# A hand-written order of attention on four engines: the turned weights' cast moved ahead of the exponentials, the queries' splits moved into other steps, the bias' scaling moved from VectorE to GpSimd

## The chip, the core and the metric

One core of a Trainium2 chip. The metric is the device time of one execution in microseconds: from the start of the program on the core to its end. Engines are named as the profile names them: PE is TensorE's matrix unit, DVE is VectorE, ACT is ScalarE, POOL is GpSimd, SP is SyncE, which here only issues DMAs.

## What is computed

A two-layer decoder trunk for one sequence of 512 tokens, 1024 features, all in float32. Layer 0 is a gated spatial mixer, a gated feed-forward part with a short convolution, and a gated embedding. Between the layers one K and V (4 heads of 64 features) is made for all later layers. Layer 1 is sliding-window attention over that K and V, then again feed-forward and embedding. The change touches only the attention of layer 1, which in the reference is:

```python
q = (xn @ w_q).reshape(B, nb, BLOCK, N_KV_HEADS, GQA_GROUP, HEAD_DIM)
scores = einsum('bnikgd,bnjkd->bnkgij', q, kblk) * HEAD_DIM ** -0.5
scores = scores - slopes * dist                  # ALiBi, one slope per query head
scores = where(valid, scores, -inf)              # a window of 128 keys
m = maximum(max(scores), sink)                   # sink: one learned logit per head
e = exp(scores - m)
probs = e / (sum(e) + exp(sink - m))
out = einsum('bnkgij,bnjkd->bnikgd', probs, vblk)
return out.reshape(B, S, 1024) @ w_o
```

There are 16 query heads in 4 groups (one per K/V head), and the 512 tokens are 4 blocks of 128. A block's queries see their own block of keys and the block before it; exactly 128 of these 256 keys are in the window.

## The kernel before, in words

**Matrix products in three passes.** [...] A product is three matmuls: high by high (L222), low by high (L223), high by low (L224). The split of a weight costs an ACT cast (`wh`, L187) and a DVE subtraction (`wl`, L196) per unit of 128x1024 numbers. Units come by DMA from SP into raw buffers (`wraw`, L166); during attention only two such buffers are in use. `pump_hi` issues the cast of the next unit, `pump` both halves.

**Attention in 16 steps.** A step i is one head group g and one block n: `steps = [(g, n) ...]`, n fastest, so steps 0, 4, 8 and 12 have n = 0 and no block of keys before them. The stages of a step are spread over three loop bodies, and within a body the order on PE, DVE, ACT and POOL is the written one (`in_order` ties each instruction to the one before it on its engine). In body i, PE does

- the scores of step i (`sc`, 8 matmuls, L741),
- the weights-by-V product of step i-2 (`pv`, 4 matmuls, or 2 where that step has n = 0, L826),
- one unit of "beside" work, then the transposes of the weights of step i-1 (`tr`, 4, L785),
- four more units of beside work.

A unit of beside work is three matmuls of 512 columns: one eighth of a half of the later groups' queries (`project`, 48 units: unit u = 15, 31 or 47 is the last of a group), or a part of the output projection (`merge`). There are 82 of them; body 0 has 7, each later body 5.

DVE does in body i: the choice between the two key blocks (`sc`, L754), scale and bias (`prs`, L755), the extreme over keys (`low`, L760: the logits are kept negated, so the minimum is the maximum of the reference), in some bodies the low half of a weight unit (`wl`), the low half of the turned weights of step i-1 (`pl`, L805), the two sums that make the output of step i-2 (`pb`, L844), which also frees the one PSUM bank that all `pv` share, and the reciprocal of the row sums (L773). ACT does the cast of a weight unit, a copy out of `pv` (L832), the four exponentials (L768), the high half of the turned weights (`ph`, L800), and the casts of the outputs (`oh`, L848). POOL masks the turned weights (L812), multiplies the weights by the reciprocal (L778), and makes the outputs' low halves (L854).

**What else stands in a body.** When a group's half of queries is projected, its split waits in the list `held`; `settle()`, late in the body, issues it: the cast `qh` on ACT (L284), the subtraction `ql` on DVE (L285) and four DMAs on SP that lay the halves out for the scores (L646, L647). Sums of the output projection into the residual (`h`, L876) wait in the same list. After steps 3, 7 and 11 the ALiBi table `alibi` (128x512) is multiplied by a constant for the next group (L915, DVE). The bodies in which a weight unit is split are those in `pumped`.

Of the kernel before, what the change touches and what calls it, by code (L numbers as in the profile page):

```python
# [18 lines left out]
NC = S // P  # L19
# [8 lines left out]
GQ = HEADS // GROUPS  # L28
# [24 lines left out]
def tile_yoco(ctx: ExitStack, tc: tile.TileContext, t, out: bass.AP, out_b: bass.AP):  # L53
    nc = tc.nc
# [98 lines left out]
    state = {"raw": 0, "unit": 0, "next": 0, "tags": list(range(RAWS)), "turn": 0, "cap": held_back}  # L153

    def load(upto, queue=nc.sync):
        while state["raw"] < min(upto, len(units)):
            j = state["raw"]
            a, m, _ = units[j]
            tags = state["tags"]
            r = wp.tile([P, UNIT], F32, tag=f"r{tags[state['turn'] % len(tags)]}", bufs=1, name=f"wraw{j}")  # L160
            state["turn"] += 1
            if len(a.shape) == 4:
                for c in range(2):
                    queue.dma_start(r[:, :m].rearrange("p (k c n) -> p k c n", c=2, n=256)[:, :, c], a[:, :, c])
            else:
                queue.dma_start(r[:, :m], a)  # L166
            raws[j] = r
            state["raw"] += 1
# [3 lines left out]
    def pump_hi(u):  # L172

        _, n, own = units[u]
        load(u + 1)
        if u not in half_done:
            if own:
                pool, *tags = own
                wh, wl = (pool.tile([P, n], F32R, tag=tg, name=f"own{u}_{tg}") for tg in tags)
            else:  # L180
                wh = wp.tile([P, UNIT], F32R, tag="wh", bufs=WBUFS, name=f"wh{u}")
                wl = wp.tile([P, UNIT], F32R, tag="wl", bufs=WBUFS, name=f"wl{u}")
            src = raws.pop(u)[:, :n]
            if u == 0:
                nc.vector.tensor_copy(wh[:, :n], src)
            else:
                nc.scalar.copy(wh[:, :n], src)  # L187
            half_done[u] = wh, wl, n, src
        return True
# [16 lines left out]
    def chunk(cols, kk, ahead=WBUFS):  # L206

        pump(state["next"] + ahead)
        parts = []
        while len(parts) < kk:  # L210
            wh, wl, n = take()
            parts += [(wh, wl, j * cols) for j in range(n // cols)]
        assert len(parts) == kk
        return parts

    def mm3(ps, parts, xs, c0, n=P, first=True, last=True):

        for k, ((wh, wl, off), (xh, xl)) in enumerate(zip(parts, xs)):
            a, b = off + c0, off + c0 + n
            st = first and k == 0  # L220
            en = last and k == len(parts) - 1
            nc.tensor.matmul(ps, wh[:, a:b], xh, start=st, stop=False)  # L222
            nc.tensor.matmul(ps, wh[:, a:b], xl, start=False, stop=False)  # L223
            nc.tensor.matmul(ps, wl[:, a:b], xh, start=False, stop=en)  # L224
# [19 lines left out]
    h = [hp.tile([P, S], F32, tag=f"h{k}", name=f"h{k}") for k in range(KD)]  # L244
# [115 lines left out]
    def slope(hd):  # L360
        return 2.0 ** (-8.0 * (hd + 1) / HEADS)
# [162 lines left out]
    for c in range(NC):  # L524
        vps[1].append(psum(f"v1_{c}"))
        mm3t(vps[1][c], xs, parts, 0, S, c)
        if c == 0:
# [24 lines left out]
                            fill=0.0, base=0, channel_multiplier=-1)  # L552
# [18 lines left out]
    for c in range(4):  # L571
# [4 lines left out]
        for j in range(2):  # L576
            m = 2 * c + j
# [3 lines left out]
            u = tp.tile([P, S], F32, tag="sg", name=f"u{m}")  # L581
# [88 lines left out]
    alibi = at.tile([P, GQ, P], F32, tag="alibi", name="alibi")  # L670
# [25 lines left out]
    box = {}  # L696

    def project(u):

        g, j, k = u // 16 + 1, u // 8 % 2, u % 8  # L700
        if u % 16 == 0:
            box["q"] = chunk(256, KD, ahead=0)
        if k == 0:
            box["qp"] = psum(f"q{g}_{j}", "mm")
        mm3(box["qp"], box["q"][k : k + 1], xq[k : k + 1], j * P, first=k == 0, last=k == KD - 1)
        if k == KD - 1:
            held.append((queries, box["qp"], g, j))

    def merge(m, k0, k1, first, last, ps=None):

        c, half = m // 2, k0 // 4
        if (c, half) not in box:
            box[c, half] = chunk(256, 4, ahead=0)
        if first:
            box[f"o{m}"] = psum(f"o{m}_{half}", "mm") if ps is None else ps
        mm3(box[f"o{m}"], box[c, half][k0 % 4 : (k1 - 1) % 4 + 1], o2[k0:k1], m % 2 * P, first=first, last=last)
        if last:
            if k0 == 3:
                held.append((nc.vector.tensor_add, h[m], h[m], box[f"o{m}"]))
            else:  # L720
                nc.vector.tensor_add(h[m], h[m], box[f"o{m}"])

# [41 lines left out]
    def exps(i, es):  # L764

        pr, low, sm = live[i]
        for e in es:
            nc.scalar.activation(pr[:, e, :], pr[:, e, :], AF.Exp, bias=low[:, e : e + 1], scale=-1.0,  # L768
                                 accum_out=sm[:, e : e + 1])

    def inverse(i):

        nc.vector.reciprocal(live[i][2], live[i][2])  # L773
# [6 lines left out]
    def turn(i):  # L780

        pr = live[i][0]
        tr = psum(f"tr{i}", "tr")
        for e in range(GQ):
            nc.tensor.transpose(tr[:, e * P : (e + 1) * P], pr[:, e, :P], ident)  # L785
        return tr

    def homes(i):

        if i % 2:  # L790
            two = [wp.tile([P, 2, S], F32R, tag=f"r{2 + q}", bufs=1, name=f"p{x}{i}") for q, x in enumerate("pm")]
            return [x[:, a, :] for x in two for a in range(2)]
        one = [ap.tile([P, S], F32R, tag=f"a{x}{SLOTS - 1}", name=f"p{x}{i}") for x in "hl"]
        m5 = mp.tile([P, 2, S], F32R, tag="m5", name=f"pm{i}") if steps[i][1] else one
        return one + ([m5[:, 0], m5[:, 1]] if steps[i][1] else one)

    def turned_hi(i, tr):

        live[i] = homes(i)
        nc.scalar.copy(live[i][0], tr)  # L800
# [53 lines left out]
            eng.tensor_sub(ol, src, oh.bitcast(F32))  # L854

    last = len(steps)
    held = []
    work = [(project, u) for u in range(48)]
    part = lambda m, k: (merge, m, k, k + 1, k == 0, k == 3 and m > 3)
    work += [part(m, k) for m, k in ((4, 0), (4, 1), (5, 0), (5, 1), (6, 0), (6, 1), (4, 2), (4, 3),  # L860
                                             (5, 2), (5, 3), (6, 2), (6, 3))]
    work += [part(m, k) for m in (7, 0, 1, 2, 3) for k in range(4)]
    work += [part(0, 4), part(1, 4)]
    beside = [work[:7]] + [work[5 * i + 2 : 5 * i + 7] for i in range(1, last)]
    assert 5 * last + 2 == len(work)
    pumped = (0, 1, 3, 4, 6, 7, 9, 10, 11, 13, 15)

    def fill(i, a, b):

        for f, *args in beside[i][a:b]:  # L870
            f(*args)

    def settle():

        for f, *args in held:
            f(*args)  # L876
        held.clear()
# [5 lines left out]
    with in_order(*engines):  # L883
        for i in range(last):
            o = scores(i)
            logits(i, o)
            cast = i and i in pumped and pump_hi(state["unit"])
            if i >= 2:
                pv = mix(i - 2)
                low = low_rows(i - 2, pv)  # L890
            if i == 0:
                values(3)
            fill(i, 0, 1)
            if i:
                tr = turn(i - 1)
            if i + 1 < last:
                sinks(i + 1)
            exps(i, (0,))
            if i:
                turned_hi(i - 1, tr)  # L900
            exps(i, (1, 2, 3))
            if cast:
                pump(state["unit"] + 1)
            if i:
                masks(i - 1, (0,))
                turned_lo(i - 1, tr)
                masks(i - 1, (1,))
            if i >= 2:
                pairs = outputs(i - 2, pv, low)
            inverse(i)  # L910
            weights(i)
            if i >= 2:
                output_lows(pairs, nc.gpsimd)
            if i % NC == NC - 1 and i + 1 < last:
                nc.vector.tensor_scalar_mul(alibi, alibi, slope(GQ - 1))  # L915
            fill(i, 1, 4)
            settle()
            if i == 0:
                pump(state["unit"] + 1)
            fill(i, 4, None)  # L920
            load(min(state["unit"] + 2, held_back))
        settle()
        pv = mix(last - 2)
        low = low_rows(last - 2, pv)
        for m in (0, 1):
            merge(m, 5, 6, False, False)
        pairs = outputs(last - 2, pv, low)
        merge(2, 4, 6, False, False)
        tr = turn(last - 1)
        turned_hi(last - 1, tr)  # L930
        masks(last - 1, (0,))
        turned_lo(last - 1, tr)
        masks(last - 1, (1,))
        output_lows(pairs, nc.gpsimd)
# [222 lines left out]
```

## Time and profile before

| | |
|---|---|
| time, median of 3 runs | 1144.59 us (1144.54 to 1144.83) |
| the profiled execution: its own time | 1144.61 us |
| its span, first to last instruction | 1142.9 us |
| mean granted TensorE clock | 0.997 |
| busy: PE, DVE, ACT, POOL | 1124.6, 736.5, 509.7, 136.3 us |
| attention, from the first scores of step 1 to the first `pv` of body 15 | 599.24 to 689.34 us |

The profile is one execution. Its own time is 1.7 us longer than its span, and 0.02 us from the median. A timeline row reads: start, duration, engine, line, operation, output<-inputs, shape, count, and in brackets the idle time before it and what ended that. Ends of matmuls are modelled, so a row of 0.39 us may be followed by the next one 0.23 us later; only starts are used here for PE.

### The profile page before, as it was taken

How to read it: one execution, taken by the hardware profiler on the slowest of the kernel's cores; microseconds unless marked ns; L12 is line 12 of the kernel's file. 1: busy time of each engine (PE TensorE's matmuls, PEld its weight loads, DVE VectorE, ACT ScalarE, POOL GpSimd, SP SyncE). 2: the span in 40 equal slices, each digit the busy share in tenths (PEclk: the TensorE clock that was granted, in tenths of full speed). 3: DMA queues.
4: the chain of work that ended last, by engine and by line, in shares of the span. 5: the costliest groups of instructions: out<-in, count | busy, mean ns of one | idle time of the engine just before them, and what ended most of it. 6: DMA issues, size and time to landing. Idle time of an engine off the chain costs nothing.

```text
span 1142.9 us, 13705 instructions
## 1 busy us (share of the span) xinstructions
PE 1124.6 (98%) x5248; PEld 937.9 (82%) x5248; DVE 736.5 (64%) x983; ACT 509.7 (45%) x808; POOL 136.3 (12%) x169
## 2 busy tenths in 40 slices
PE   9999999999999999999999999999999999999996
PEld 7888888888888888888897788888888888888895
DVE  7356467762677367557857886687735774577656
ACT  6533344441343244445756766554423442344532
POOL 2100210000000000022233453200000000000232
PEclk9999999999999999999999999999999999999998
DMA  9322322322323333332054324432322323332202
GB/s 319 123 82 81 104 88 97 111 92 92 108 71 99 111 110 86 100 111 93 19 147 129 103 65 167 141 107 84 111 92 93 102 73 104 110 97 88 81 13 74
DMA packets 44690, 116.48 MB, mean 102 GB/s; under 512 B 4936, under 2 KB 16848, under 8 KB 44624
## 3 DMA queue, kind: packets, MB, share of 16 engines
q1 hardware_dynamic: 43504, 114.42, 31.6%
q10 hardware_dynamic: 1120, 1.18, 0.3%
q8 instruction: 41, 0.67, 0.2%
q14 instruction: 25, 0.20, 0.1%
HBM read 108.24 MB, written 2.11 MB: 97 GB/s over the span
## 4 chain that ended last, share of the span: by engine, by line
PE 90%; DVE 5%; ACT 2%; issue 1%; POOL 1%; DMA 0%; SPq 0%; POOLq 0%; DVEq 0%; ACTq 0%
PE up L224 14%; PE up L223 14%; PE up L222 14%; PE d L223 8%; PE d L224 8%; PE d L222 8%; PE gate L222 2%; PE gate L224 2%; PE gate L223 2%; PE u L224 1%; PE u L222 1%; PE u L223 1%; PE v L234 1%; PE v L233 1%; PE v L235 1%
## 5 line engine op out<-in xcount | busy, mean ns | idle before, releaser
L196 DVE TENSOR_TENSOR wl<-wraw,wh 128x1024 fp32r<-128x1024 f32 (+2 forms) x197 | 237.5, 1207 | 121.8 <-ACT wh L187 121.2
L187 ACT CAST wh<-wraw 128x1024 fp32r<-128x1024 f32 (+1 forms) x196 | 201.8, 1032 | 235.5 <-PE d L223 135.9
L222 PE MATMUL up<-nf00h,wh 128*128 128x512 f32 x352 | 137.1, 390 | 0.0
L222 PE MATMUL up<-nf10h,wh 128*128 128x512 f32 x352 | 137.0, 389 | 0.0
L224 PE MATMUL up<-nf00h,wl 128*128 128x512 f32 x352 | 137.0, 389 | 0.0
L223 PE MATMUL up<-nf10l,wh 128*128 128x512 f32 x352 | 136.9, 389 | 0.0
L222 PE MATMUL d<-ah,wh 128*128 128x512 f32 x352 | 136.9, 389 | 0.0
L223 PE MATMUL d<-al,wh 128*128 128x512 f32 x352 | 136.9, 389 | 0.0
L224 PE MATMUL d<-ah,wl 128*128 128x512 f32 x352 | 136.9, 389 | 0.0
L223 PE MATMUL up<-nf00l,wh 128*128 128x512 f32 x352 | 136.9, 389 | 0.0
L224 PE MATMUL up<-nf10h,wl 128*128 128x512 f32 x352 | 136.9, 389 | 0.0
L409 ACT ACTIVATE c<-hs,vec 128x512 f32<-128x512 f32 x88 | 71.6, 814 | 88.2 <-DVE hs L405 87.2
L410 DVE SCALAR_TENSOR_TENSOR c<-hs,vec,c 128x511 f32<-128x511 f32 x88 | 65.9, 749 | 37.4 <-ACT c L409 37.2
L383 DVE TENSOR_TENSOR h<-h,d 128x512 f32<-128x512 f32 x56 | 38.5, 687 | 69.0 <-PE d L224 69.0
L284 ACT CAST ah<-a 128x512 fp32r<-128x512 f32 x44 | 27.3, 622 | 113.4 <-DVE a L415 113.4
L222 PEld LDWEIGHTS up<-nf10h,wh 128*128 128x128 f32 x352 | 66.1, 188 | 13.8
L223 PEld LDWEIGHTS up<-nf00l,wh 128*128 128x128 f32 x352 | 66.1, 188 | 13.8
L222 PEld LDWEIGHTS d<-ah,wh 128*128 128x128 f32 x352 | 66.1, 188 | 13.8
L223 PEld LDWEIGHTS d<-al,wh 128*128 128x128 f32 x352 | 66.1, 188 | 13.7
L223 PEld LDWEIGHTS up<-nf10l,wh 128*128 128x128 f32 x352 | 66.1, 188 | 13.7
L224 PEld LDWEIGHTS up<-nf00h,wl 128*128 128x128 f32 x352 | 66.1, 188 | 13.7
L224 PEld LDWEIGHTS d<-ah,wl 128*128 128x128 f32 x352 | 66.1, 188 | 13.7
(316 smaller groups left out, 2027.9 us busy)
## 6 DMA issues: line engine op xcount, KB each, us to landing
wraw<-in_w_up SPq DMA_DIRECT2D x88, 512.0 KB, 3.5
wraw<-in_w_down SPq DMA_DIRECT2D x32, 512.0 KB, 3.6
wraw<-in_w_down SPq DMA_DIRECT2D x16, 384.0 KB, 3.3
wraw<-in_w_u SPq DMA_DIRECT2D x8, 512.0 KB, 6.8
wraw<-in_w_out SPq DMA_DIRECT2D x8, 512.0 KB, 3.7
wraw<-in_w_gate SPq DMA_DIRECT2D x8, 512.0 KB, 4.0
wraw<-in_w_q SPq DMA_DIRECT2D x8, 512.0 KB, 3.5
wraw<-in_w_o SPq DMA_DIRECT2D x8, 512.0 KB, 3.3
```

What stands on the lines that cost most here:

```text
L187: nc.scalar.copy(wh[:, :n], src)
L196: nc.vector.tensor_sub(wl[:, :n], src, wh[:, :n].bitcast(F32))
L222: nc.tensor.matmul(ps, wh[:, a:b], xh, start=st, stop=False)
L223: nc.tensor.matmul(ps, wh[:, a:b], xl, start=False, stop=False)
L224: nc.tensor.matmul(ps, wl[:, a:b], xh, start=False, stop=en)
L233: nc.tensor.matmul(ps, xh[:, s], wh[:, a:b], start=st, stop=False)
L234: nc.tensor.matmul(ps, xl[:, s], wh[:, a:b], start=False, stop=False)
L235: nc.tensor.matmul(ps, xh[:, s], wl[:, a:b], start=False, stop=en)
L284: nc.scalar.copy(hi, src)
L383: nc.vector.tensor_add(h[m], h[m], ps)
L409: nc.scalar.activation(c, hs, AF.Identity, bias=v("conv_b", l * 2 * NJ + col), scale=cw[2])
L410: nc.vector.scalar_tensor_tensor(c[:, 1:], hs[:, : S - 1], cw[1], c[:, 1:], op0=ALU.mult, op1=ALU.add)
```

## The change

In the bodies with a weight split nothing is settled any more. In the others (2, 5, 6, 8, 10, 12) `settle()` comes directly behind `logits`, so behind `low`. The last half of the first projected group (u = 15) is settled where it is projected, in body 2. The high half `ph` of step i-1 is written ahead of all four exponentials of step i, instead of behind the first. The `alibi` multiplication goes to GpSimd, ahead of the sinks and the masks of its body. `pumped` loses the effective entries 6 and 10 and gains 14. The sums into `h` have a list of their own and come one per body at the end. Body 0 has 8 units of beside work and body 15 has 4.

```diff
@@ project
         if k == KD - 1:
             held.append((queries, box["qp"], g, j))
+            if u == 15:
+                settle()
@@ merge
             if k0 == 3:
-                held.append((nc.vector.tensor_add, h[m], h[m], box[f"o{m}"]))
+                sums.append((h[m], h[m], box[f"o{m}"]))
@@
-    beside = [work[:7]] + [work[5 * i + 2 : 5 * i + 7] for i in range(1, last)]
-    assert 5 * last + 2 == len(work)
-    pumped = (0, 1, 3, 4, 6, 7, 9, 10, 11, 13, 15)
+    beside = [work[:8]] + [work[5 * i + 3 : 5 * i + 8] for i in range(1, last)]
+    pumped = (1, 3, 4, 7, 9, 11, 13, 14, 15)
@@ the loop over steps
             logits(i, o)
-            cast = i and i in pumped and pump_hi(state["unit"])
+            if i in pumped:
+                pump_hi(state["unit"])
+            elif i > 1:
+                settle()
...
             if i:
                 tr = turn(i - 1)
+                turned_hi(i - 1, tr)
+            if i % NC == NC - 1 and i + 1 < last:
+                nc.gpsimd.tensor_scalar_mul(alibi, alibi, slope(GQ - 1))
             if i + 1 < last:
                 sinks(i + 1)
-            exps(i, (0,))
-            if i:
-                turned_hi(i - 1, tr)
-            exps(i, (1, 2, 3))
-            if cast:
+            exps(i, range(GQ))
+            if i in pumped:
                 pump(state["unit"] + 1)
...
-            if i % NC == NC - 1 and i + 1 < last:
-                nc.vector.tensor_scalar_mul(alibi, alibi, slope(GQ - 1))
-            fill(i, 1, 4)
-            settle()
+            fill(i, 1, None)
             if i == 0:
                 pump(state["unit"] + 1)
-            fill(i, 4, None)
+            if sums:
+                nc.vector.tensor_add(*sums.pop(0))
             load(min(state["unit"] + 2, held_back))
-        settle()
+        assert not sums and not held
```

**DVE, from the end of body 4 into body 5** (the digits behind a name are the step: `sc5`, `low5`; `ql2_0` is the low half of the first half of group 2's queries). Before:

```order
L773 RECIPROCAL sm4_4907<-sm4_4907 128x4
L285 TENSOR_TENSOR ql2_0_4957<-q2_0_4822,qh2_0_4956 128x512
L754 COPY_PREDICATED sc5_4971<-above_467,sc5_4971 128x4x128
L755 SCALAR_TENSOR_TENSOR prs_4587<-sc5_4971,rq_4382,alibi_4491 128x4x128
L760 TENSOR_REDUCE low5_4982<-prs_4587 128x4
L805 TENSOR_TENSOR pl4_5003<-tr4_4995,ph4_5002 128x512
L844 TENSOR_TENSOR pb3_4990<-pv3_4985,pb3_4990 64x2x128 x2
```

After, at the same place:

```order
L775 RECIPROCAL sm4_4910<-sm4_4910 128x4
L756 COPY_PREDICATED sc5_4964<-above_467,sc5_4964 128x4x128
L757 SCALAR_TENSOR_TENSOR prs_4587<-sc5_4964,rq_4382,alibi_4491 128x4x128
L762 TENSOR_REDUCE low5_4975<-prs_4587 128x4
L285 TENSOR_TENSOR ql2_0_4979<-q2_0_4822,qh2_0_4978 128x512
L807 TENSOR_TENSOR pl4_5004<-tr4_4998,ph4_5003 128x512
L846 TENSOR_TENSOR pb3_4993<-pv3_4988,pb3_4993 64x2x128 x2
```

The queries' low half has moved from ahead of the logits of step 5 to behind its `low`.

**ACT, body 5.** Before:

```order
L284 CAST qh2_0_4956<-q2_0_4822 128x512
L832 COPY pb3_4990<-pv3_4985 64x512
L768 ACTIVATE prs_4587,sm5_4984<-prs_4587,low5_4982 128x129
L800 CAST ph4_5002<-tr4_4995 128x512
L768 ACTIVATE prs_4587,sm5_4984<-prs_4587,low5_4982 128x129 x3
```

After:

```order
L284 CAST qh2_0_4978<-q2_0_4822 128x512
L834 COPY pb3_4993<-pv3_4988 64x512
L802 CAST ph4_5003<-tr4_4998 128x512
L770 ACTIVATE prs_4587,sm5_4977<-prs_4587,low5_4975 128x129 x4
L850 CAST oh0_4794<-pb3_4993 128x128
```

`ph4` now stands ahead of all four exponentials of step 5; it used to stand behind the first, which waits for `low5`.

**ACT, body 15, the last one** (`wh121`, `wh122`: weight units of the output projection). Before:

```order
L187 CAST wh122_5667<-wraw122_5462 128x1024
L832 COPY pb13_5675<-pv13_5670 64x512
L768 ACTIVATE prs_4587,sm15_5666<-prs_4587,low15_5664 128x129
L800 CAST ph14_5686<-tr14_5680 128x512
L768 ACTIVATE prs_4587,sm15_5666<-prs_4587,low15_5664 128x129 x3
```

After:

```order
L187 CAST wh121_5666<-wraw121_5581 128x1024
L834 COPY pb13_5674<-pv13_5669 64x512
L187 CAST wh122_5756<-wraw122_5650 128x1024
L802 CAST ph14_5684<-tr14_5679 128x512
L770 ACTIVATE prs_4587,sm15_5665<-prs_4587,low15_5663 128x129 x4
```

One unit fewer has been split by then, and its cast (issued by the code behind the loop, and placed here by the scheduler) stands ahead of `ph14` and the exponentials of step 15.

More of the change, by code (lines that the diff above doesn't have):

```diff
@@ L856, in tile_yoco @@
     last = len(steps)
-    held = []
+    held, sums = [], []
     work = [(project, u) for u in range(48)]
```

## The prediction, made before the changed kernel ran

> **What bounds the kernel now.** I read the page first, then the chain of waits, then a table of windows over the attention, then the timeline.
>
> ```profile
> PE 1124.6 (98%) x5248; PEld 937.9 (82%) x5248; DVE 736.5 (64%) x983; ACT 509.7 (45%) x808; POOL 136.3 (12%) x169
> ...
> PE 90%; DVE 5%; ACT 2%; issue 1%; POOL 1%; DMA 0%; SPq 0%; POOLq 0%; DVEq 0%; ACTq 0%
> ```
>
> PE bounds nearly everything, and the change takes nothing from it. What can be won lies where the chain leaves PE: 5% of it is on DVE and 2% on ACT, much of that between 600 and 672 us, in the attention. PE's "busy" hides its waits there, since the ends of matmuls are modelled. So I cut the stage at the first scores of bodies 2 to 15; the last window ends at the first `pv` of body 15's tail. Columns: from:to, length, busy time of PE, PEld, DVE, ACT, POOL, clock, DMA.
>
> ```profile
> 604.10:609.46 5.36, 5.36 (x31) 4.45 (x29) 3.21 (x6) 2.85 (x10) 1.18 (x2) 1.00 0.67 196
> 609.46:615.98 6.52, 5.98 (x33) 4.97 (x31) 5.32 (x9) 4.61 (x15) 3.29 (x6) 1.00 0.27 62
> 615.98:622.68 6.70, 6.10 (x33) 5.00 (x31) 6.30 (x12) 5.32 (x19) 4.03 (x8) 1.00 0.31 99
> 622.68:628.45 5.77, 5.77 (x32) 4.91 (x31) 3.50 (x7) 2.92 (x10) 2.56 (x5) 1.00 0.66 183
> 628.45:634.64 6.19, 5.66 (x31) 4.51 (x30) 5.83 (x11) 5.41 (x20) 2.95 (x6) 1.00 0.03 5
> 634.64:640.43 5.79, 5.79 (x32) 4.91 (x31) 4.61 (x8) 3.88 (x11) 2.49 (x6) 1.00 0.60 171
> 640.43:646.74 6.31, 6.10 (x32) 5.00 (x31) 4.57 (x9) 3.42 (x13) 3.16 (x6) 1.00 0.65 175
> 646.74:653.43 6.69, 6.01 (x32) 4.96 (x31) 6.18 (x11) 5.61 (x20) 3.28 (x6) 1.00 0.07 17
> 653.43:658.76 5.33, 5.33 (x31) 4.53 (x30) 4.15 (x8) 3.71 (x9) 2.05 (x5) 1.00 0.63 175
> 658.76:665.20 6.44, 6.03 (x33) 4.97 (x32) 5.83 (x10) 4.75 (x17) 3.75 (x7) 1.00 0.27 84
> 665.20:671.14 5.94, 5.90 (x33) 4.92 (x32) 4.72 (x10) 2.64 (x10) 2.79 (x6) 1.00 0.25 88
> 671.14:677.78 6.64, 6.02 (x33) 4.97 (x32) 6.21 (x11) 5.26 (x19) 3.27 (x6) 1.00 0.00 1
> 677.78:683.08 5.30, 5.30 (x30) 4.45 (x29) 3.55 (x8) 3.13 (x12) 2.61 (x5) 1.00 0.32 99
> 683.08:689.34 6.26, 6.21 (x33) 5.00 (x32) 5.78 (x12) 4.82 (x18) 3.81 (x7) 1.00 0.38 107
> ```
>
> Every body from 2 to 14 gives PE the same work, but for half a `pv` in bodies 2, 6, 10, 14 and narrower scores in 4, 8, 12. Undisturbed, it takes 5.78 us (bodies 5 and 7), or 5.33 with half a `pv` (2, 10, 14). I use 5.78 for 4, 8, 12 too, since none of these is undisturbed. What is above that: 0.74 (body 3), 0.92 (4), 0.86 (6), 0.53 (8), 0.91 (9), 0.66 (11), 0.16 (12), 0.86 (13): **5.64 us of waits**, all that an order can win here. Why they arise is seen at body 5 into 6, in rows of three engines:
>
> ```profile
> 623.37 0.50 ACT L848 CAST oh<-pb 128x128 fp32r<-128x128 f32 x2 [0.40 <-DVE pb L844]
> ...
> 624.38 0.69 DVE L285 TENSOR_TENSOR ql<-q,qh 128x512 fp32r<-128x512 f32 x1 [0.90 <-ACT qh L284]
> ...
> 624.99 0.69 DVE L754 COPY_PREDICATED sc<-above,sc 128x512 f32<-128x512 uint32 x1
> ...
> 627.36 0.41 ACT L768 ACTIVATE prs<-prs,low 128x129 f32<-128x129 f32 x1 [2.03 <-DVE low L760]
> ...
> 627.88 0.59 ACT L800 CAST ph<-tr 128x512 fp32r<-128x512 f32 x1
> ...
> 628.50 0.69 DVE L805 TENSOR_TENSOR pl<-tr,ph 128x512 fp32r<-128x512 f32 x1 [1.17 <-ACT ph L800]
> ...
> 629.11 0.84 DVE L844 TENSOR_TENSOR pb<-pv,pb 64x256 f32<-64x256 f32 x2
> ...
> 630.09 0.47 PE L826 MATMUL pv<-ph,vt 128*128 128x512 f32 x1 [0.53 <-DVE pb L844]
> ```
>
> DVE loses time twice. It waits 0.90 us for `qh` ahead of the next logits, and 1.17 us for `ph`, which stands behind an exponential that needs `low`. `pb` therefore ends at 629.95, and PE's next `pv`, which needs the bank that `pb` frees, starts 0.14 later, at 630.09.
>
> **The change, part by part.** Whether the waits go is a race of DVE against PE. DVE in body 6, with a weight split and no queries' split ahead of it, and two rows on PE's pace:
>
> ```profile
> 630.07 0.67 DVE L754 COPY_PREDICATED sc<-above,sc 128x512 f32<-128x512 uint32 x1
> ...
> 632.31 1.22 DVE L196 TENSOR_TENSOR wl<-wraw,wh 128x1024 fp32r<-128x1024 f32 x1
> 633.57 0.69 DVE L805 TENSOR_TENSOR pp<-tr,pp 128x512 fp32r<-128x512 f32 x1
> 634.18 0.83 DVE L844 TENSOR_TENSOR pb<-pv,pb 64x256 f32<-64x256 f32 x2
> ...
> 678.92 0.70 DVE L754 COPY_PREDICATED sc<-above,sc 128x512 f32<-128x512 uint32 x1 [0.33 <-PE sc L741]
> ...
> 684.03 0.47 PE L826 MATMUL pv<-pp,vt 128*128 128x512 f32 x1
> ```
>
> From a body's first scores, T, the logits can start at T+1.14 (677.78 to 678.92) and `pb` is done 4.94 later (630.07 to 635.01); with 0.14 for the signal the next `pv` is free at T+6.22. PE asks for it 0.95 behind the next first scores (683.08 to 684.03): at T+6.73, or T+6.28 after half a `pv`. So **with a weight split DVE is 0.51 us early, or 0.06 in body 14**. With a queries' split in its place (0.69 for 1.22) it is 1.04 early, 0.59 in bodies 6 and 10.
>
> *Queries' splits behind `low`* (bodies 2, 5, 6, 8, 10): the 0.90 wait for `qh` and the 0.69 ahead of the logits go; `ql` fills time in which DVE had nothing to do.
>
> *`ph` ahead of the exponentials*: the 1.17 goes, since the transposes end before `low` does. What is late next is `ql` or `wl`, already in the sum. The four exponentials then wait for `ph`, 0.59 long; only the reciprocal and POOL's product wait for them (third rival).
>
> *u = 15 in body 2*: that body has two queries' splits, and the second still stands ahead of body 3's logits. `pb` ends at T+5.55, and from there to the logits it takes 1.71, as above from 623.28 to 624.99 (`oh` starts 0.09 behind `pb`). So the logits come at T+7.26 instead of T+6.50 (5.36+1.14): 0.76 late, 0.51 of it covered. **0.25 us stays in body 4.** Their DMAs:
>
> ```profile
> L647 SPq DMA_DIRECT2D q<-ql x16: 461/587/1300, 583.3 to 656.4; - x16
> ...
> DMA to landing us min/median/max: 2.2/2.3/3.0
> ```
>
> Behind `ql`, SP issues three more at 0.59 (1.30 at worst), and the last lands 2.3 later: T+10.7 to 11.5. Its scores are due at T+11.7 (5.36+5.78+0.6): no wait, by little. Other queries' DMAs are due a body or more later.
>
> *`alibi` on POOL*, in bodies 3, 7 and 11. DVE loses 0.40 each, which the sum above does not contain. POOL has no such row:
>
> ```profile
> L915 DVE TENSOR_SCALAR alibi<-alibi 128x512 f32<-128x512 f32 x3 | 1.2, 397 | 0.0
> ...
> L729 POOL TENSOR_SCALAR alibi<-dist x4: 636/1034/1165, 21.2 to 24.1; 128x128 f32<-128x128 f32 x4
> ...
> 598.22 1.04 POOL L778 TENSOR_TENSOR prs<-prs,sm 128x512 f32<-128x512 f32 x1 [1.96 <-DVE sm L773]
> ...
> 598.90 1.44 DVE L196 TENSOR_TENSOR wl<-wraw,wh 128x1024 fp32r<-128x1024 f32 x1 [0.76 <-ACT wh L187]
> ...
> L812 POOL TENSOR_SCALAR_AFFINE_SELECT pm<-pp 128x512 fp32r<-128x512 f32 x16 | 10.2, 635 | 20.4 <-ACT pp L800 19.7
> ```
>
> Bounds: 0.64 us (L812, the same size) to 4.1 (four times L729's quarter). I take 1.04, L778's, the nearest in size. It starts at T+2.7, when the biased logits are done, and ends at T+3.75; behind it stand the sinks, the masks and the product, none due before T+6. At 1.04 POOL costs nothing by itself. But it meets `wl`, due at T+3.38 (632.31 less 630.07, plus 1.14). A `wl` beside L778 took 1.44 instead of 1.22. I add 0.25 to each of the three; 0.51 covers it in bodies 7 and 11, nothing does in body 3: **0.25 us more in body 4.**
>
> [...]
>
> *Sums into `h`*: the same four, one a body:
>
> ```profile
> L876 DVE TENSOR_TENSOR h<-h,o 128x512 f32<-128x512 f32 x4 | 2.6, 670 | 0.0
> ```
>
> In bodies 11 and 13 they follow `wl`: 4.94+0.20+0.67 = 5.81 against 5.78. Nothing. The units of beside work number 82 as before: PE's sum is unchanged. In body 15 the cast of a late unit stands ahead of `ph`; its DMA may hold ACT. I count nothing, and up to 0.8 in the range. The loads of the next stage wait one split longer, behind PE work of several us: nothing.
>
> **Sum**: 5.64 less 0.50 is 5.1 us. From the profiled execution's 1144.61 (span 1142.9 and 1.7 around it), which is the median of the runs within 0.02: **1139.5 us**.
>
> **The rivals.** (1) *POOL is slow*: at 4.1 us `alibi` ends at T+6.8, the sinks (0.2) and two masks at T+8.27. The last row of `pv` needs them at T+7.43: 0.84 us in three bodies, 2.5 in all: 1142.0. For it: L729. Against it: L729's rows ran while DVE worked too, and the other 128x512 rows take 0.64 and 1.04.
>
> (2) *The bank stays last*: `wl` and `ql` stand ahead of `pl` and `pb`, so if each DVE body grows by 1.0 us (three rows blocked for 0.33) beside a POOL that works at other moments than before, the six bodies with a weight split whose margin is 0.51 cost 0.49 each and body 14 costs 0.94: 3.9 in all, 1143.4. For it: the margins are small. Against it: in body 14 of before, with nothing ahead of its logits, DVE waits for PE (678.92, 0.33).
>
> (3) *The exponentials wait for PE*, and it gets slower: they now follow `ph`, which follows the transposes, which follow the product of the step before on POOL, which follows its exponentials: a loop. Transposes 0.4, `ph` 0.6, exponentials 1.8, reciprocal 0.4, product 1.2: 4.4 us against 5.33 to 5.78. It decides from 0.9 us more; at 6.4 us each of 14 bodies gains 0.6 over PE's pace: 1144.6-5.6+8.4 = 1147.4. For it: ACT runs in order. Against it: the sum.
>
> The change doing something other than it says isn't one: the order of the instructions was read above.
>
> **How the numbers follow.** Forecast 0.80, (1) 0.08, (2) 0.08, (3) 0.04. Low end: all 5.64, 0.2 for the narrow scores and 0.2 in body 15: 1138.6. High end: POOL's upper bound, 1142.0. A measurement tells 0.2% (2.3 us) from no change; (2) lies within it, and half of (1) may: faster 0.84, same 0.12, slower 0.04.
>
> **What would show it.** Right: bodies near 5.78 and 5.33 but for body 4 (some 6.2); `pl` no longer waits for `ph`; PE's wait for `pb` all but gone; the stage ends 5 us earlier and everything behind keeps its length. Wrong: POOL's `alibi` rows over 2 us, exponentials ended by `ph`, bodies still at 6.2 and more, or a wait of PE behind the attention that wasn't there.

## The result and the profile after

The changed kernel takes **1139.31 us** (median of 5, 1138.97 to 1139.68) against 1144.59 (median of 5, 1144.54 to 1145.04) of the kernel before: a ratio of 0.9953, 95% interval 0.9938 to 0.9967. That is 5.28 us less; 1139.5 was forecast, inside 1138.6 to 1142.0. Its profiled execution has a span of 1137.5 us and a granted clock of 0.997, as before.

First the page: the busy times, and the shares of the chain by engine.

```profile
PE 1122.8 (99%) x5248; PEld 938.6 (83%) x5248; DVE 733.6 (64%) x980; ACT 509.2 (45%) x808; POOL 145.1 (13%) x172
...
PE 95%; DVE 1%; issue 1%; POOL 1%; ACT 1%; DMA 1%; SPq 0%; POOLq 0%; ACTq 0%; DVEq 0%
```

PE's work is the same, DVE's 5% of the chain has become 1%. Then the windows from first scores to first scores, bodies 2 to 15 (from:to, length, busy time of PE, PEld, DVE, ACT, POOL, clock, DMA).

```profile
604.88:610.21 5.33, 5.33 (x31) 4.53 (x29) 4.43 (x9) 3.55 (x13) 2.38 (x4) 1.00 0.51 151
610.21:615.98 5.77, 5.77 (x33) 4.91 (x32) 4.63 (x8) 4.68 (x14) 4.27 (x7) 1.00 0.59 136
615.98:621.92 5.94, 5.92 (x33) 4.93 (x32) 5.72 (x11) 4.26 (x14) 4.53 (x8) 1.00 0.26 99
621.92:627.68 5.76, 5.76 (x32) 4.91 (x31) 4.49 (x10) 3.94 (x15) 2.01 (x5) 1.00 0.52 148
627.68:633.01 5.33, 5.33 (x30) 4.54 (x29) 3.96 (x7) 3.58 (x13) 3.21 (x6) 1.00 0.34 80
633.01:638.78 5.77, 5.77 (x33) 4.91 (x32) 4.70 (x9) 4.18 (x13) 4.90 (x8) 1.00 0.23 54
638.78:644.49 5.71, 5.71 (x33) 4.86 (x31) 4.76 (x10) 3.88 (x14) 3.44 (x7) 1.00 0.49 146
644.49:650.26 5.77, 5.77 (x33) 4.91 (x32) 4.07 (x6) 4.11 (x13) 2.02 (x4) 1.00 0.12 30
650.26:655.55 5.29, 5.29 (x31) 4.49 (x29) 4.65 (x10) 3.81 (x13) 3.18 (x6) 1.00 0.51 151
655.55:661.34 5.79, 5.79 (x33) 4.91 (x32) 5.32 (x10) 4.17 (x13) 4.94 (x8) 1.00 0.23 56
661.34:667.05 5.71, 5.71 (x32) 4.85 (x31) 5.03 (x11) 3.63 (x15) 3.49 (x8) 1.00 0.21 82
667.05:672.82 5.77, 5.77 (x33) 4.91 (x32) 4.76 (x8) 3.76 (x12) 1.94 (x4) 1.00 0.03 6
672.82:678.14 5.32, 5.32 (x30) 4.53 (x29) 4.93 (x9) 4.29 (x13) 3.76 (x6) 1.00 0.25 94
678.14:684.27 6.13, 6.13 (x34) 4.94 (x32) 5.55 (x12) 5.18 (x15) 3.80 (x6) 1.00 0.54 192
```

All bodies now have PE's own length, 5.77 or 5.33, and 5.71 with narrow scores (8, 12); only body 4 is longer, by 0.23. What became of the place that the prediction took apart, body 5 into 6, is seen in the timeline:

```profile
625.92 0.68 DVE L807 TENSOR_TENSOR pl<-tr,ph 128x512 fp32r<-128x512 f32 x1
626.52 0.84 DVE L846 TENSOR_TENSOR pb<-pv,pb 64x256 f32<-64x256 f32 x2
...
628.63 0.40 PE L828 MATMUL pv<-ph,vt 128*128 128x512 f32 x1
628.83 0.70 DVE L756 COPY_PREDICATED sc<-above,sc 128x512 f32<-128x512 uint32 x1 [1.26 <-PE sc L743]
```

`pl` waits for nothing, `pb` ends at 627.36, 1.27 ahead of the `pv` that needs its bank, and DVE then waits 1.26 for PE's scores. Before, PE waited for DVE here.

### The profile page after: what moved, and what is told of

It reads as the page before. It is cut to its first block, busy times and chain, and to the rows that moved or that the text cites. A ratio compares the mean times of both kernels' runs of the same rounds, so it can differ in the third digit from the quotient of the medians.

```text
span 1137.5 us, 13704 instructions
## 1 busy us (share of the span) xinstructions
PE 1122.8 (99%) x5248; PEld 938.6 (83%) x5248; DVE 733.6 (64%) x980; ACT 509.2 (45%) x808; POOL 145.1 (13%) x172
## 4 chain that ended last, share of the span: by engine, by line
PE 95%; DVE 1%; issue 1%; POOL 1%; ACT 1%; DMA 1%; SPq 0%; POOLq 0%; ACTq 0%; DVEq 0%
PE up L222 14%; PE up L224 14%; PE up L223 14%; PE d L224 8%; PE d L222 8%; PE d L223 8%; PE gate L222 2%; PE gate L223 2%; PE gate L224 2%; PE q L222 1%; PE q L224 1%; PE sc L743 1%; PE q L223 1%; PE u L222 1%; PE u L224 1%; PE u L223 1%
## 5 line engine op out<-in xcount | busy, mean ns | idle before, releaser
L224 PEld LDWEIGHTS up<-nf10h,wl 128*128 128x128 f32 x352 | 66.1, 188 | 13.7
```

## The experiments

None of the twelve kernels leaves out a part of the reference. "Alone" kernels start from the kernel before, "undone" ones from the kernel after. Before, run beside them on the same chips, took 1144.68 to 1144.76 us. The lengths of bodies below are read from the timelines, first scores to first scores; bold is 0.2 or more above PE's own length.

| kernel | time, us | 3 | 4 | 6 | 7 | 8 | 9 | 10 | 11 | 12 | 13 |
|---|---|---|---|---|---|---|---|---|---|---|---|
| before | 1144.59 | **6.52** | **6.70** | **6.19** | 5.79 | **6.31** | **6.69** | 5.33 | **6.44** | **5.94** | **6.64** |
| e1 ph alone | 1140.97 | 5.77 | **6.22** | 5.31 | 5.76 | **6.48** | 5.79 | 5.32 | **6.45** | 5.72 | 5.76 |
| e2 queries alone | 1141.96 | 5.84 | **6.69** | 5.33 | **6.30** | 5.70 | 5.77 | 5.32 | **6.31** | **5.98** | **6.60** |
| e11 both, old schedule | 1140.00 | 5.76 | **6.24** | 5.33 | **6.29** | 5.72 | 5.76 | 5.33 | **6.33** | 5.71 | 5.77 |
| e3 schedule alone | 1144.88 | **6.54** | **6.68** | **6.19** | **6.99** | 5.72 | **6.09** | 5.32 | **6.76** | 5.72 | **6.00** |
| e4 ph undone | 1140.46 | 5.83 | **6.67** | 5.32 | 5.82 | 5.71 | 5.75 | 5.43 | 5.76 | 5.72 | 5.76 |
| e5 queries undone | 1139.10 | 5.77 | 5.76 | 5.32 | 5.77 | 5.71 | 5.77 | 5.29 | 5.78 | 5.79 | 5.77 |
| after | 1139.31 | 5.77 | **5.94** | 5.33 | 5.77 | 5.71 | 5.77 | 5.29 | 5.79 | 5.71 | 5.77 |

**e1: ph alone.** In the kernel before:

```diff
-            exps(i, (0,))
             if i:
                 turned_hi(i - 1, tr)
-            exps(i, (1, 2, 3))
+            exps(i, range(GQ))
```

> The kernel before with one edit: the high half of the turned weights is written ahead of all four exponentials. Theory (DVE against PE, a margin per body): in a body with a weight split the 1.22 us of wl cover the 1.17 us that pl waits for ph, so the edit wins nothing there (bodies 3, 7, 10, 11: the waits in the bodies behind them, 0.92, 0.53, 0.66 and 0.16, stay). In the bodies without one (2, 5, 8, 12) it wins the 1.17, and the waits of bodies 3, 6, 9 and 13 (0.74, 0.86, 0.91, 0.86: 3.4 together) go. So 1141.2 us, 1140.6 to 1142.0. Rival 1 (the gain comes from where the weight splits stand): within 0.5 of 1144.6. Rival 2 (this move is the whole gain): 1139.3.

1140.97 us (ratio 0.9966, 0.9954 to 0.9979), inside the range. The waits of bodies 3, 6, 9 and 13 are gone and 11's is there, as the theory has it; 12's 0.16 went too. Bodies 4 and 8 still wait, but not for the theory's reason alone. Body 4 has 0.51 over 5.71 (0.99 before), and `wl` of the weight split ahead of it takes 1.66 instead of 1.22, beside a mask on POOL that started 0.05 ahead:

```profile
613.71 0.63 POOL L812 TENSOR_SCALAR_AFFINE_SELECT pm<-ph 128x512 fp32r<-128x512 f32 x1 [1.34 <-ACT ph L800]
613.76 1.66 DVE L196 TENSOR_TENSOR wl<-wraw,wh 128x1024 fp32r<-128x1024 f32 x1
```

In body 8 (0.77 over 5.71, 0.60 before) PE stands 0.39 in the scores for the DMA that lays out `ql`, until 639.85; `pb` comes last all the same, at 640.12. One moved cast is worth 3.7 of the 5.3 us, and what it wins lies behind the bodies without a weight split.

**e2: the queries' splits alone.** In the kernel before:

```diff
             logits(i, o)
+            if i > 1:
+                settle()
...
-            settle()
+            for s in sums:
+                nc.vector.tensor_add(*s)
+            sums.clear()
```

> The kernel before with one part of the change: the queries' splits go directly behind low (u = 15 stays in body 2), the sums into h keep their place in a list of their own, all else is as before. Theory: DVE is no longer late for the logits; ql fills 0.69 of the 1.17 wait for ph where no weight is split. In bodies 3, 6, 7 and 10 ql and wl then stand in one body, and DVE ends 0.69 later than with wl alone: against margins of 0.51 (0.06 behind the short bodies 6 and 10) that is 0.2 in 4 and 8 (0.25 more in 4 for u = 15) and 0.6 in 7 and 11, some 1.9 us in all of the 5.64. So 1140.9 us, 1140.3 to 1141.7. Rival 1 (the gain comes from where the weight splits stand): within 0.5 of 1144.6. Rival 2 (the move of ph is the whole gain): 1144 and more.

1141.96 us (0.9977, 0.9968 to 0.9986), 0.3 above the range. 7 and 11 wait about as worked out (0.5 each, against 0.6), and the 0.2 of body 8 did not come. Body 4 waits 0.98 against 0.45: `pp` of body 2 still waits 0.64 for its high half, as in e4 below, and that moves the logits of body 3. 12 waits 0.27 and 13 still 0.83, which the estimate had left out: body 12 has neither a weight split nor queries' splits, so nothing fills the wait of `pl` for `ph`, and two sums into `h` and the bias stand at the end of body 11.

**e3: the schedule alone.** The kernel after with the three moves undone; the places of units, weight splits and sums remain.

```diff
-            elif i > 1:
-                settle()
...
-                turned_hi(i - 1, tr)
-            if i % NC == NC - 1 and i + 1 < last:
-                nc.gpsimd.tensor_scalar_mul(alibi, alibi, slope(GQ - 1))
...
-            exps(i, range(GQ))
+            exps(i, (0,))
+            if i:
+                turned_hi(i - 1, tr)
+            exps(i, (1, 2, 3))
...
+                nc.vector.tensor_scalar_mul(alibi, alibi, slope(GQ - 1))
-            fill(i, 1, None)
+            fill(i, 1, 4)
+            settle()
+            fill(i, 4, None)
```

> The kernel after with three parts undone: ph behind the first exponential, the queries' splits at the end of the body, the bias' multiplication on DVE. What is left of the change is where units of beside work and weight splits stand and the sums into h one by one. Theory: logits late by 0.6 to 0.9 and pl by 1.17 in bodies 2, 5, 6, 8 and 10, together about 1.8 to 2.1 against a margin of 1.73 without a weight split (1.28 behind short bodies 2, 6, 10): 0.3 to 0.8 in each of the bodies 3, 6, 7, 9, 11 and 0.3 in body 4. So 1142.3 us, 1141.3 to 1143.5. Rival (the gain comes from this schedule): 1139.3 to 1139.7.

1144.88 us (1.0002, 0.9992 to 1.0011): no gain at all. The rival falls; the theory's figure was 2.6 too low. The kernel of before shows why: its logits of body 5 stand at T+2.31 (624.99 less 622.68), 1.17 late, not the 0.6 to 0.9 that I had used, and 1.17 for `ph` comes on top.

**e4: ph undone** (the exponentials' lines as in e3, nothing else).

> The kernel after with one part undone: ph behind the first exponential again. Theory: with the queries' splits behind low, pl is late by 1.17 less 0.69 in the bodies with ql (0.48 against 1.04, 0.59 behind the short ones), not at all behind wl, and by 1.17 in body 12 (against 1.73). No margin is used up: 1139.3 us, 1139.0 to 1139.7, all bodies at the lengths of the kernel after. Rival 2 (the move of ph is the gain, or half of it): 1142 to 1144.6, with waits of 0.5 to 0.9 in most bodies.

1140.46 us (0.9963, 0.995 to 0.9976): 0.8 above the range, and nearly all of it in one body. DVE in bodies 2 and 3 of e4, then of the kernel after (the timeline):

```profile
609.63 0.69 DVE L807 TENSOR_TENSOR pp<-tr,pp 128x512 fp32r<-128x512 f32 x1 [0.64 <-ACT pp L802]
...
612.18 0.69 DVE L285 TENSOR_TENSOR ql<-q,qh 128x512 fp32r<-128x512 f32 x1 [0.90 <-ACT qh L284]
612.79 0.69 DVE L756 COPY_PREDICATED sc<-above,sc 128x512 f32<-128x512 uint32 x1
```

```profile
611.43 0.69 DVE L285 TENSOR_TENSOR ql<-q,qh 128x512 fp32r<-128x512 f32 x1 [0.90 <-ACT qh L284]
612.04 0.69 DVE L756 COPY_PREDICATED sc<-above,sc 128x512 f32<-128x512 uint32 x1
```

The 0.64 that `pp` waits in body 2 moves the second queries' split and the logits of body 3 from 612.04 to 612.79, and body 4 grows by 0.73. Elsewhere the margins hold, as expected; I had forgotten that body 3 has none left.

**e5: the queries' splits undone** (as the `settle` lines of e3, and no `settle` in `project`).

> The kernel after with one part undone: the queries' splits at the end of a body again, ahead of the next logits (ends of bodies 1, 2, 4, 5, 7, 9). Theory: with ph ahead of the exponentials, logits that come 0.8 to 1.2 late are covered where no weight is split (margin 1.73, 1.28 behind a short body), and the only weight split behind a late one is that of body 3. The kernel with ph alone has the same three splits around body 3 and waits 0.51 in body 4, against 0.23 in the kernel after. So 0.3 more: 1139.6 us, 1139.2 to 1140.0. Rival (the queries' move has a gain of its own, in each of six bodies): 1141 and more, waits in bodies 6, 9 and 11.

1139.10 us (0.9949, 0.9933 to 0.9965): 0.1 below the range, and no slower than the kernel after; the 0.3 more that was worked out from e1 did not come (e10 shows why). With `ph` moved and the weight splits placed as they are, the queries' move wins nothing; body 4 is even 0.18 shorter, since `u = 7` no longer stands in the middle of body 2.

**e6: the bias on DVE.**

```diff
-            if i % NC == NC - 1 and i + 1 < last:
-                nc.gpsimd.tensor_scalar_mul(alibi, alibi, slope(GQ - 1))
...
+            if i % NC == NC - 1 and i + 1 < last:
+                nc.vector.tensor_scalar_mul(alibi, alibi, slope(GQ - 1))
```

> The kernel after with one part undone: the bias' multiplication on DVE, behind the reciprocal of bodies 3, 7 and 11. Theory: 0.40 at the end of DVE's body makes the logits of bodies 4, 8 and 12 that much later at most, against margins of 0.44 (weight split and narrow scores), 0.97 and 1.66: 1139.3 us, 1139.0 to 1139.6, bodies 5, 9 and 13 at 5.76 to 5.86. Rival (DVE's time is what is short, so the 1.2 us count): 1140.5.

1139.83 us (0.9955, 0.9941 to 0.997), 0.2 above the range; bodies 5, 9 and 13 at 5.76 to 5.77, as the theory has it, but body 4 at 6.23, which neither theory has. The timeline of body 3, POOL and DVE:

```profile
613.57 0.63 POOL L814 TENSOR_SCALAR_AFFINE_SELECT pm<-ph 128x512 fp32r<-128x512 f32 x1 [1.38 <-ACT ph L802]
613.78 1.50 DVE L196 TENSOR_TENSOR wl<-wraw,wh 128x1024 fp32r<-128x1024 f32 x1
```

The mask starts 0.21 ahead of `wl`, and `wl` takes 1.50 instead of 1.22. In the kernel after, POOL is busy with the bias then, and the mask comes later. e10 tests that.

**e10: bias on DVE, and a multiplication by 1.0 on POOL at the old place** (one line more than e6).

```diff
+                nc.gpsimd.tensor_scalar_mul(alibi, alibi, 1.0)
```

> The kernel with the bias' multiplication on DVE, and at the place where POOL had it a multiplication by 1.0 on POOL. In the kernel with the multiplication on DVE, body 4 waited 0.52 instead of 0.23, and wl in body 3 took 1.50 instead of 1.22 beside POOL's mask that had started 0.2 ahead of it. Theory (the multiplication on POOL is worth something because it holds that mask back until wl is done): wl in body 3 takes 1.22 again and body 4 5.94 to 6.0. Rival (what counts is DVE's 0.40): body 4 stays at 6.23.

1139.15 us (0.9954, 0.994 to 0.9967), body 4 at 5.95. The same place:

```profile
613.23 1.49 POOL L902 TENSOR_SCALAR alibi<-alibi 128x512 f32<-128x512 f32 x1 [1.10 <-DVE prs L757]
613.85 1.22 DVE L196 TENSOR_TENSOR wl<-wraw,wh 128x1024 fp32r<-128x1024 f32 x1
...
615.07 0.63 POOL L814 TENSOR_SCALAR_AFFINE_SELECT pm<-ph 128x512 fp32r<-128x512 f32 x1
```

`wl` is back at 1.22 and body 4 at its length, though DVE does the 0.40 in three bodies. So DVE's 1.2 us cost nothing; POOL's multiplication was worth 0.29 us in body 4 because it keeps the mask off `wl`. The mask became able to meet `wl` when `ph` moved ahead: 0.44 of the 0.51 that body 4 waits in e1 is this stretch of `wl`. In e5 POOL has the bias and `wl` takes 1.22, so e1's 0.51 was the wrong thing to reckon e5 from.

**e7: a dose for the margins.** `pl` is subtracted twice:

```diff
         nc.vector.tensor_sub(pl, tr, ph.bitcast(F32))
+        nc.vector.tensor_sub(pl, tr, ph.bitcast(F32))
```

> The kernel after with the subtraction pl done twice in every body (same data, 0.62 us more of DVE each): a dose for the margins. Theory (margins 0.44 to 0.51 with a weight split, 0.06 behind body 14, 1.0 with a queries' split and 0.59 behind short ones, none in body 3): waits of 1.4 in body 4 (now 0.23; bodies 2 and 3 add up), 0.1 to 0.2 each in 5, 8, 10, 12 and 14, 0.6 in the tail of 15, next to nothing in 6, 7, 9, 11. Some 2.7 us: 1142.0, 1141.2 to 1142.9. Rival 1 (DVE is as full as PE: each body pays in full): 8 us, 1147.4. Rival 2 (margins over 0.62 everywhere): 1139.3.

1145.40 us (1.0008, 0.9999 to 1.0017), 2.5 above the range. The dose was larger than meant: in body 7 the two rows start at 639.11 and 639.82, 0.71 apart. Against the kernel after, the first `pv` of bodies 8, 10, 12 and 14, each behind a weight split, starts 0.23, 0.12, 0.33 and 0.12 later in its body: 0.38 to 0.59 of the dose was covered. The bodies themselves grow by 0.27, 0.32, 0.34 and 0.29; what they have beyond the wait comes behind the `pv`. Bodies 5, 6, 9, 11 and 13 grow by nothing or 0.02 at most, body 7 by 0.11, body 2 by 0.19, body 4 by 1.28, and in body 15 the first `pv` comes 1.1 later (there `wl` of body 14 took 1.60, beside a mask). So neither rival: there are margins, and they are small. Some 2 us more arise behind the loop, which no theory had. There the last transposes (693.68) are followed directly by the `pv` that needs their weights (694.96), where eight other matmuls stand between the two in the kernel after (688.40 to 690.31). Why the order differs is open; the whole time of e7 is therefore no measure of the margins.

**e9: the bias three times on POOL.**

```diff
                 nc.gpsimd.tensor_scalar_mul(alibi, alibi, slope(GQ - 1))
+                nc.gpsimd.tensor_scalar_mul(alibi, alibi, 1.0)
+                nc.gpsimd.tensor_scalar_mul(alibi, alibi, 1.0)
```

> The kernel after with the bias' multiplication on POOL followed by two more by 1.0: POOL's price three times, at the same place. Theory A (1.49 us is the operation's own price on POOL): 4.47 us; in body 3 it ends at T+7.9, the masks at T+8.8 and T+9.4, so body 4 grows to 7.9; in bodies 7 and 11 the masks end at T+8.05 and T+8.7 against a need at T+6.97 and T+7.43, so bodies 8 and 12 grow to 7.0. Together 4.6 us: 1143.9, 1143.0 to 1144.8. Theory B (its own price is near 0.64 and DVE beside it stretches it): the two more take 0.64 each, all three 2.8: bodies 4, 8 and 12 grow by 0.2 at most, 1139.6.

1145.54 us (1.0009, 1.0 to 1.0018; its executions scatter from 1144.48 to 1146.88), 0.7 above the range. The rows of the tile `alibi` (ns, minimum, median and maximum of three):

```profile
L902 POOL TENSOR_SCALAR alibi<-alibi x3: 1489/1492/1493, 614.1 to 664.0; 128x512 f32<-128x512 f32 x3
L903 POOL TENSOR_SCALAR alibi<-alibi x3: 1611/1613/1614, 615.6 to 665.6; 128x512 f32<-128x512 f32 x3
L904 POOL TENSOR_SCALAR alibi<-alibi x3: 1488/1488/1489, 617.3 to 667.3; 128x512 f32<-128x512 f32 x3
```

Theory A: the third runs while DVE waits for it, and takes 1.49 all the same, so that is its own price. In the profiled execution bodies 4, 8 and 12 grow to 9.51, 7.39 and 7.41, where 7.9, 7.0 and 7.0 were expected; what body 4 has beyond that is told in the last section.

**e11: both moves, old schedule** (e1's and e2's edits together).

> The kernel before with ph ahead of the exponentials and the queries' splits behind low, while the weight splits, the sums into h and the units of beside work stay where they were. Theory (where wl and ql stand in one body DVE is too long by 0.2 to 0.6, whatever the order inside): of the waits with the queries' move alone (0.98 in body 4, 0.53 in 7, 0.53 in 11, 0.27 in 12, 0.83 in 13) that of 13 goes and that of 4 falls by 0.5, the others stay: 1140.6 us, 1140.2 to 1141.2. Rival (the two moves add up, the schedule is worth nothing): 1139.3.

1140.00 us (0.996, 0.9945 to 0.9976): 12 and 13 are mended, 4 in part, and 7 and 11 wait 0.5 as with e2. There `ql` and `wl` stand in one body (6 and 10), and neither move mends that. So the total is 0.2 below the range. The rest of the change wins 0.7 us on this kernel: 1.06 in bodies 7 and 11 by the schedule, 0.30 in body 4, less 0.59 that is lost behind the loop (told at e8). The 0.30 is the place of the bias: as in e6, `wl` of body 3 takes 1.50 here beside the mask. Alone the schedule won nothing.

**e8 and e12: the leftovers mended.** In both a weight split in body 12 as well; in e8 `settle` also in body 1, in e12 the queries' splits as in e5.

```diff
-    pumped = (1, 3, 4, 7, 9, 11, 13, 14, 15)
+    pumped = (1, 3, 4, 7, 9, 11, 12, 13, 14, 15)
...
-            elif i > 1:
+            if i == 1 or i not in pumped:
                 settle()
```

> The kernel after with its two leftovers mended: settle also in body 1 (the split of u = 7 leaves body 2), and a weight split in body 12 as well (the unit that was split behind the loop is then split in body 15, and the embedding's units are loaded and cast earlier). Theory: body 4 at 5.71 instead of 5.94; the wait of 0.47 at the embedding's first matmuls, whose low halves DVE ended late, goes; the split in body 12 uses up to 0.2 in the tail of 15. So 1138.75 us, 1138.4 to 1139.1. Rival (the split in body 12 with the sum into h behind it is one too many: DVE 5.81 against 5.71 in 12, and so on to 14): waits of 0.3 or more in 13 to 15, 1139.3 and more.

> The kernel after with the queries' splits at the end of their bodies again and a weight split in body 12 as well. Theory: body 4 at 5.76 as with the queries' splits undone, no wait of 0.47 at the embedding's first matmuls: 1138.6 us, 1138.2 to 1139.1, as fast as with both leftovers mended. Rival (the queries' move is worth something once all else is mended): 1139.1 and more.

e8 takes 1138.59 us (0.9948, 0.9934 to 0.9962), e12 1138.43 (0.9947, 0.9934 to 0.9959): both 0.7 to 0.9 below the kernel after, and as fast as each other within their scatter (1138.20 to 1139.36, 1138.24 to 1138.61). Body 4 is 5.73 and 5.76; in e8 body 2 is 0.07 longer instead. The second leftover lies behind the loop, at the embedding's first matmuls. First of the kernel before, where nothing waits, then after, then e8 (timeline):

```profile
698.38 0.28 PE L222 MATMUL o<-own_m,wh 128*128 128x256 f32 x1
...
701.18 0.28 PE L222 MATMUL pin<-own_m,wh 128*128 128x256 f32 x1
```

```profile
690.12 1.05 ACT L187 CAST wh<-wraw 128x1024 fp32r<-128x1024 f32 x1
...
691.69 1.48 DVE L196 TENSOR_TENSOR wl<-wraw,wh 128x1024 fp32r<-128x1024 f32 x1
...
692.63 0.28 PE L222 MATMUL o<-own_m,wh 128*128 128x256 f32 x1
692.74 0.28 PE L223 MATMUL o<-own_m,wh 128*128 128x256 f32 x1
693.22 0.39 PE L224 MATMUL o<-own_m,wl 128*128 128x256 f32 x1 [0.20 <-DVE wl L196]
...
696.02 0.28 PE L222 MATMUL pin<-own_m,wh 128*128 128x256 f32 x1
```

```profile
685.90 1.05 ACT L187 CAST wh<-wraw 128x1024 fp32r<-128x1024 f32 x1
...
692.40 0.28 PE L222 MATMUL o<-own_m,wh 128*128 128x256 f32 x1
...
695.20 0.28 PE L222 MATMUL pin<-own_m,wh 128*128 128x256 f32 x1
```

From `o` to `pin` it is 2.80 us before, 3.39 after, 2.80 in e8. With one split more inside the loop the embedding's unit is cast at 685.90 instead of 690.12, its low half is there in time, and 0.59 us come back.

## Why the prediction was right, point by point

**The waits.** 5.64 us of waits in bodies 3 to 13, made by DVE and mended by the order: right, in size and in place. The undisturbed lengths were 5.77 and 5.33. For bodies 4, 8 and 12 they are 5.71, so 0.07 each was won beyond what was counted. One thing was overlooked, in body 4 of the kernel before (timeline):

```profile
617.27 0.30 PE L741 MATMUL sc<-kh,q 128*128 128x128 f32 x1 [0.51 <-DMA q<-ql]
...
617.77 0.47 PE L826 MATMUL pv<-ph,vt 128*128 128x512 f32 x1
```

The scores themselves waited, for the DMA of a queries' half that was split late: they went on 0.68 later than in the kernel after. `pb` ended at 617.62 and still came last, so the account of 5.64 holds, but a second wait lay hidden behind it. In e1 it shows in body 8; in the kernel after, e2, e3, e5 and e11 no scores wait 0.1 or more for this DMA.

**Two causes.** Both delays were real, but they are not two gains. e1 and e2 win 3.7 and 2.7 by themselves, e11 4.7; in the final schedule the queries' move is worth nothing (e5) and that of `ph` 1.15 (e4). A body without a weight split has room for one delay, not for two; a body with one hides the wait for `ph` behind `wl`. The prediction gave the sum rightly and did not see that either cause could be left in nearly everywhere.

**The margin of 0.51 with a weight split.** About right. In the kernel after, `pb` ends, with the 0.14 for the signal, 0.49, 0.51 and 0.59 us ahead of the first `pv` of bodies 8, 12 and 14; e7 gives 0.38 to 0.59. In body 10 it is only 0.25, since DVE stands idle for 0.46 ahead of `low` of step 9, for a reason that the profile doesn't show. In body 15 it is 0.15 where 0.06 was worked out.

**u = 15 in body 2: 0.25 us in body 4.** 0.23 was measured, with some luck. `ql` waits 0.90 for `qh` at 611.43 and the logits of body 3 start at 612.04, T+7.16 against T+7.26 worked out: 0.69 late instead of 0.76. With the 0.49 of body 8 as the room, 0.20 is left; `pv` comes 0.18 later than in body 8. e5 and e8 show the better wording: two queries' splits in body 2 are one too many; with one, body 4 has 0.02 to 0.05.

**The bias on POOL: 1.04 us and 0.25 for a collision.** This step failed in both numbers. The operation takes 1.49, and the collision did not come (the timeline of the kernel after, body 3):

```profile
613.66 1.49 POOL L902 TENSOR_SCALAR alibi<-alibi 128x512 f32<-128x512 f32 x1 [1.10 <-DVE prs L757]
614.29 1.22 DVE L196 TENSOR_TENSOR wl<-wraw,wh 128x1024 fp32r<-128x1024 f32 x1
615.12 0.43 POOL L748 COPY prs<-nsink 128x4 f32<-128x4 f32 x1
```

`wl` ran 0.86 us beside the multiplication, which ended at 615.15, and took its usual 1.22. What was late is POOL's own next row, the sinks: 0.43 instead of 0.19, ended at 615.55, 0.04 behind `wl`. In e6 it was `wl` that took 0.28 longer, behind a mask that had 0.42 left. The 0.25 was taken from the product L778: beside it, lead and stretch of `wl` together are 0.90 (598.22, 598.90 and 0.22 longer). Beside the multiplication they are only 0.47 (last section), and here it started 0.63 ahead. POOL needs 1.49 for what DVE did in 0.40. POOL had the time, so the price was without effect; the place on POOL helped by chance (e6, e10).

**Sums into h, body 15: nothing.** Right: bodies 12 and 14, behind those with a sum and a split, are 5.71 and 5.32, and PE's gap at the last `pv` of body 15 is 0.14 (0.21 before).

**The loads of the next stage: nothing, behind PE work of several us.** This step failed: 0.59 us. I looked at how long PE had work, and not at what stands ahead of the late unit's cast on ACT and of its subtraction on DVE: `pp`, the other unit, and then 1.48 us of `wl`.

**The sum.** From the first scores of body 0 to the embedding's `o` it is 107.69 us before (590.69 to 698.38) and 101.84 after (590.79 to 692.63): 5.85 less. 5.64, 0.21 for the narrow scores and less 0.23 make 5.62 of it; the rest is in gaps of under 0.1. Then 0.59 goes back: 5.26, and 5.28 was measured. That the forecast of 5.1 was so near is in part luck: one loss too many (0.25) and gains not counted (0.2) stood against a loss that was overlooked (0.59).

**The rivals.** POOL at 4.1 us or more does cost what was said and more (e9: with 4.6 us the bodies 4, 8 and 12 grow by 1.7 to 3.6, since the logits of the next body wait for the bias too). The bank comes last again from some 0.4 to 0.6 us more of DVE (e7); the second rival's 1.0 us a body, three rows blocked for 0.33, was my assumption and no run shows it: beside a mask or the multiplication `wl` was stretched by at most 0.44 (e1). The third rival's wait did appear, in the kernel after too (body 5):

```profile
624.72 0.69 DVE L762 TENSOR_REDUCE low<-prs 128x4 f32<-128x516 f32 x1
625.12 0.59 ACT L802 CAST ph<-tr 128x512 fp32r<-128x512 f32 x1 [0.55 <-PE tr L787]
625.60 0.41 ACT L770 ACTIVATE prs<-prs,low 128x129 f32<-128x129 f32 x1
```

`ph` waits 0.55 for PE's transposes, and the exponentials follow it, 0.19 behind the end of `low`; in bodies 4, 7, 8, 11, 12 and 13 it is 0.12 to 0.34. It cost nothing: these bodies keep PE's length, but for what body 4 has from elsewhere. So of the signs of being wrong two came up, exponentials released by `ph` and a new wait of PE behind the attention, and only the second cost time.

## What to carry to other kernels

Lay out the race that sets a stage per step: when the fast engine asks, when the slow one answers, and how much room is left in each kind of step; two delays that share one room are worth one gain, so leave-one-out runs say more than the sum of the parts. Spread optional work so that no step holds two pieces of it, and look at the first rows behind the stage as closely as at the stage. Count what a moved instruction keeps its engine from doing at that moment, too.

## What the runs showed of the hardware

Where the subtraction `wl` on DVE overlapped a mask, the multiplication or the product on POOL, the row that started first kept its usual time; how much longer the later one took went with the lead of the first. In e7, body 7, the bias' multiplication starts only 0.37 ahead of `wl`, and `wl` takes 1.32 instead of 1.22 (timeline):

```profile
637.50 1.49 POOL L903 TENSOR_SCALAR alibi<-alibi 128x512 f32<-128x512 f32 x1
637.87 1.32 DVE L196 TENSOR_TENSOR wl<-wraw,wh 128x1024 fp32r<-128x1024 f32 x1
```

Lead and stretch together are 0.47 here, and 0.47 in e4 (body 7: 0.42 and 0.05). For masks they are 0.49 in e1 (0.05 and 0.44) and in e6 (0.21 and 0.28), and 0.50 in e7 (body 14: 0.12 and 0.38). With a lead of 0.6 neither a mask (e11, body 6) nor the multiplication (after, e10) stretches `wl`. So by estimate from these rows `wl` is put off until 0.47 to 0.50 us after the start of either, though one takes 0.63 and the other 1.49. The other way round, a mask that starts together with `wl` takes 1.71 (after, body 14, both at 676.22), as long as `wl` and 0.49 more. No run was made to test this; it is read from rows that happened to differ.

In the profiled execution of e9 PE's granted clock was 0.50 behind a wait of 2 us. PE stood for a mask until 619.59; its last matmul had started at 617.40, and at 0.23 a matmul that is a wait of 1.96 (the profile counts 1.73 as idle). The windows behind it (length, busy times, clock, DMA):

```profile
619.59:622.32 2.73, 2.73 (x7) 2.04 (x8) 2.59 (x4) 0.58 (x1) 2.73 (x4) 0.50 0.00 0
...
645.27:648.00 2.73, 2.73 (x13) 2.02 (x14) 2.10 (x4) 1.03 (x2) 2.50 (x5) 1.00 0.38 86
```

For 2.73 us the granted clock was 0.50, and matmuls of 512 columns started every 0.43 us instead of 0.23. The next window, from 622.32 to 626.60, shows 0.92; if the clock there was 0.50 and then 1.00, it was 0.50 until 623.0, 3.4 us in all, which by estimate cost half of that, 1.7 us: nearly as much as the wait itself. The second window, behind a wait of 1.46 us in body 8, shows 1.00, and so do the 2.74 us behind a wait of PE that the profile counts as 1.79 in the kernel after (1091.56 to 1094.30). So the half clock came behind one wait of this length and not behind another, and what decides it is not shown. Nor is it shown whether it came in every execution of e9: five of the ten take 1145.85 to 1146.88 us at a mean clock of 0.996, the other five 1144.48 to 1145.23 at 0.997, and the one trace is of the first five.
